# A hybrid decoder block on one core: pieces of work moved, another end, and two K steps of the second MLP product split earlier into general-pool tiles

## The chip, the core and the metric

The kernel runs on one core of one Trainium2 chip. The metric is the device time of one execution in microseconds, smaller is better. The engines of the core are named as in the profile: PE (TensorE, the matmuls), DVE (VectorE), ACT (ScalarE), POOL (GpSimd) and SP (SyncE, which here only issues DMAs). Operands that PE and the other engines work on lie in on-chip memory (SBUF), sums of products in PSUM; the rest moves by DMA.

## The reference

One layer of a pre-norm decoder block, on x of 1 x 2048 x 1024 in float32:

```python
h = rmsnorm(x, norm_mix_g)
u = h @ w_in                                   # 1024 -> 3*512 + 2*1024 columns
gate_b, gate_c, v, x_r, g = split(u)
y_conv = gate_b * causal_dwconv(gate_c * v, conv_w)            # width 512, 3 taps
xr = causal_dwconv(x_r, rnn_conv_w) + rnn_conv_b               # width 1024, 4 taps
y_rnn = rg_lru(xr, w_a, b_a, w_x, b_x, lru_lambda) * gelu(g)   # a scan over the sequence
y = concat(rmsnorm(y_conv, g_norm_conv), rmsnorm(y_rnn, g_norm_rnn))
x = x + y @ w_out                                              # 1536 -> 1024
h = rmsnorm(x, norm_mlp_g)
z = square(relu(h @ w_mlp_in))                                 # 1024 -> 4096
x = x + z @ w_mlp_out                                          # 4096 -> 1024
out = rmsnorm(x, final_norm_g)
```

## The kernel before

**Precision.** Every float32 operand of a large product is split into a high part (rounded to a shorter format, a cast on ACT, L172) and a low part (what is left, a subtraction on DVE, L173). A product is three matmuls: high by high, high by low, low by high. So each weight or operand tile of 128 x 1024 costs one cast of ACT and one subtraction of DVE before PE can use it. `round_off` and `split_new` do this.

**Blocks.** The sequence is four blocks of 512 rows, taken two at a time: `b` is 0 and then 2. Each pass has the stages mixers, `w_out` product, first MLP product ("up"), second MLP product ("down"). The pass with `b` = 0 computes the mixers with plain products (`mixers_plain`), the pass with `b` = 2 with block products (`mixers_blocks`). From the second pass on, and in both MLP products, the two blocks and two halves of the other sides are multiplied by a scheme of seven block products in place of eight: the products are numbered 1 to 7 and run in the order `ORDER = (1, 2, 6, 5, 7, 3, 4)`, with sums and differences of operands made on DVE. H1 to H7 are the operands of the first MLP product, made once per pass; `ops.put` makes H7, H3 and H4.

**Who sets the order.** The kernel is written for a framework that lays out each engine's instructions at build time: a planner takes them in the order of the program text as priority, as far as its own model finds them ready, and each engine then runs its list strictly in that order. Inside `tc.manual_schedule(engines=...)` the named engines keep the order of the text itself. PE is listed there from the `w_out` products on; in the mixers of the first pass it is not. `tc.issue_after(ins)` puts the instructions of its body behind `ins` on the same engine.

**Memory.** SBUF tiles come from pools with a fixed number of slots: the general pool (`temp`, 23 slots), the weight pool (`wtile`, 15 slots) and a pool of four wide tiles (`wide` and `duo`). A tile that finds no free slot waits for the last reader of an older one. PSUM has four tiles of 128 x 2 x 512.

**The places that the change touches, in order of time.**

- The start (`mixers_plain`, n = 0): row factors of the first norm are not applied to x before the product but to the product's result. `firsts[k].factors()` makes them for block k, `spread` turns them into a 128 x 512 tile with a diagonal (L362), a matmul with ones (L370) and a copy by ACT (L405); then `drain_x` and `drain_g` multiply the PSUM tiles by it (L720, L723).
- The end of the first mixers: `w_out_conv` multiplies the conv half of y, 4 row tiles per block. Between its tiles `during(t)` runs other work: for t = 0 it fetches the y of the second block (`fetch_y`), runs `between(0)`, which is the gate (sigmoids on ACT) and the scan of the last unit, and splits the fetched y (`conv_operands`, L652 and L653).
- The gate group of the second mixers (`InGate`): `refill_u` loads the tile `u1` from DRAM into a wide slot.
- The first MLP product: step n multiplies pair (s, i) of `seq`, `drain` takes it out of PSUM (L1065 to L1106) and spills z to DRAM; weights are prepared two steps ahead. The first six steps are i = 1 and 2 for s = 0, 1, 2; steps 6 to 10 are 6, 5, 7, 3, 4 of s = 0. In steps 2, 3 and 4 H7, H3 and H4 are made.
- The second MLP product: `Down.fetch` loads z and the weights of one of the 56 K steps, `prepare` splits them, `multiply` runs 24 matmuls. The first two are prepared in the last two steps of the first product, behind their drains, into weight-pool tiles.
- The end (`b` = 2): the last two K steps are multiplied row tile by row tile; each tile is added to x (L1549), squared and summed by ACT (L1206), its factor is made by `rstd_of` and both halves are scaled by DVE (L1220) and written out.

Of the kernel before, what the change touches and what calls it, by code (L numbers as in the profile page):

```python
# [10 lines left out]
AF = mybir.ActivationFunctionType  # L11
# [3 lines left out]
P = 128  # L15
# [46 lines left out]
def block_kernel(  # L62
# [257 lines left out]
    def rstd_of(dst, v, n):  # L320
        a = small("rs_a")[:, :n]
        s = small("rs_s")[:, :n]
        q = small("rs_q")[:, :n]
        V.tensor_scalar(a, v, 1.0 / D, EPS, MUL, ADD)
        root = nc.scalar.activation(s, a, AF.Sqrt)
        V.reciprocal(s, s)
        if n == 1:
            V.scalar_tensor_tensor(q, s, a, s, MUL, MUL)
        else:
            V.tensor_mul(q, s, s)  # L330
            V.tensor_mul(q, q, a)
        V.tensor_scalar(q, q, -0.5, 1.5, MUL, ADD)
        V.tensor_mul(dst, s, q)
        return root.ins

    HALF = [slice(0, 512), slice(512, D)]

# [343 lines left out]
    def mixers_plain(h):  # L681
# [30 lines left out]
        for n in SEQUENCE:  # L712
            if n < 4:
                pr = n
                u0, u1 = Lru(2 * pr), Lru(2 * pr + 1)
                xin = new_xin(pr)
                g = wide("g")

                def drain_x(blk, ps):
                    V.tensor_mul(block(xin, blk, 3), ps, over(R, blk))  # L720

                def drain_g(blk, ps):
                    V.tensor_mul(block(g, blk), ps, over(R, blk))  # L723
                    nc.scalar.activation(block(g, blk), block(g, blk), AF.Gelu_apprx_tanh)

                if pr == 0:
                    pss = []
                    wg = both("g0", lambda blk, ps: pss.append(ps), (0,))
                    with tc.issue_after(prepare_second()):
                        for k in range(4):  # L730
                            firsts[0].part(k)
                    firsts[0].factors()
                    both("x0", lambda blk, ps: pss.append(ps), (1,), w_first)
                    psR = psum("bc")
                    firsts[0].spread(R[:, 0, :], psR[:, 0, :])
                    seen = nc.gpsimd.tensor_copy(warm, R[:, 0, 0:1]).ins
                    with tc.issue_after(seen):
                        for m, i, pair in held:
                            kept[m, i] = [spill_r("ws", t, nc.gpsimd) for t in pair]
                    split_kept = spilled[0]  # L740
                    drain_x(0, start_x)
                    for k in range(4):
                        firsts[1].part(k)
                    firsts[1].factors()
                    pss.append(
                        col_products(
                            "g0", wg, h[1], lambda: firsts[1].spread(R[:, 1, :], psR[:, 1, :])
                        )
                    )
                    drain_x(1, pss[1])  # L750
                    drain_g(0, pss[0])
                else:
                    around("x%d" % pr, drain_x, late)
                    wg = None
                gw = load_gate(pr)
                keep_halo(pr, xin)
                u0.conv(xin)
                if late:
                    late.out()
                if pr == 3:  # L760
                    fetched = [fetch_y(mix.ys["A"], q, 0) for q in range(2)]
                if pr:
                    wg = both("g%d" % pr, drain_g, (0,), take("g%d" % pr, 1 + pr // 3))
                u1.conv(xin)
                last = latest[0]
                if pr == 3:
                    keep_sums(n)
                    rA = stats(mix.acc["A"], 512, "A")
                if pr:
                    both("g%d" % pr, drain_g, (1,), wg)  # L770
                else:
                    drain_g(1, pss[2])
                if pr == 3:
                    ysA = conv_operands(fetched)
                if pr:
                    u0.gate(gw)
                    u0.scan()
                late = Late(mix, u0, u1, g, gw)
                if pr < 3:
                    with tc.issue_after(last), tc.issue_after(split_kept):  # L780
                        keep_sums(n)
                continue
            if n < 6:
                pr = n - 4
                if R2 is None:
                    R2 = temp("R2")
                    nc.scalar.activation(R2, R, AF.Square)
                gc = wide("gc")
                around(
                    "c%d" % pr,  # L790
                    lambda blk, ps: V.tensor_mul(block(gc, blk), ps, over(R2, blk)),
                    late,
                )
                if late:
                    late.out()
                    late = None
                cv = new_cv(pr)
                both(
                    "v%d" % pr,
                    lambda blk, ps: V.tensor_mul(block(cv, blk, 2), ps, block(gc, blk)),  # L800
                )
                u = conv_short(pr, cv)
                for blk in range(2):
                    V.tensor_mul(block(u, blk), block(u, blk), over(R, blk))
                us[pr] = spill("u", u, nc.gpsimd)
                for k in range(4):
                    nxt[pr].part(k)
                nxt[pr].factors()
            else:
                for pr in range(2):  # L810
                    u = refill_u(us[pr])
                    around(
                        "b%d" % pr, lambda blk, ps: V.tensor_mul(block(u, blk), ps, block(u, blk)), late
                    )
                    if late:
                        late.out()
                        late = None
                    mix.conv(u)
            keep_sums(n)
# [109 lines left out]
    class InGate(In):  # L929

        def drain(self, i):
# [15 lines left out]
            elif i == 2:  # L947
                gated(self.u0, 0, plus(block(self.t, 0), self.y))
            elif i == 6:
                self.u1 = refill_u(self.us[1])  # L950
                snap(block(self.t, 1), self.x)
            elif i == 5:
                snap(block(self.t, 0), self.w)
            elif i == 7:
                gated(self.u1, 1, plus(block(self.t, 0), self.x))
# [176 lines left out]
    class Down:  # L1132
# [14 lines left out]
            else:  # L1147
                load(t, W2[a, i])

        def prepare(self, i, a):  # L1150
            self.ready[i, a] = (
                split_new(self.z.pop((i, a)), wtile, "z"),
                split_new(self.w.pop((i, a)), wtile, "w"),
            )

        def multiply(self, i, a, ts=range(NT)):
# [48 lines left out]
            sq = temp("sq", (P, TB))  # L1205
            nc.scalar.activation(sq, x_half(b, t, i), AF.Square, accum_out=ss[:, i : i + 1])  # L1206

    def finish_tile(b, t, gfin, ss=None, queues=None):
        rs = small("rs")[:, 0:1]
        if ss is None:  # L1210
            ss = small("ss")
            finish_squares(b, t, ss, range(2))
        else:
            finish_squares(b, t, ss, (0,))
        V.tensor_add(ss[:, 0:1], ss[:, 0:1], ss[:, 1:2])
        rstd_of(rs, ss[:, 0:1], 1)
        r0 = b * TB + t * P
        for i, sl in enumerate(HALF):
            xv = x_half(b, t, i)
            V.scalar_tensor_tensor(xv, xv, rs, gfin[:, sl], MUL, MUL)  # L1220
            (queues or (nc.gpsimd, nc.gpsimd))[i].dma_start(outf[r0 : r0 + P, sl], xv)

    def finish(b):
        gfin = gain(final_norm_g)
# [112 lines left out]
    for b in range(0, NB, 2):  # L1337
# [8 lines left out]
        with tc.manual_schedule(engines={nc.tensor.engine}):  # L1346
# [1 line left out]
            ahead = 0 if b else 1  # L1348
            ws = [take("oA0", ahead), take("oA1", ahead)]

            nextA = []

            def during(t):
                if t == 0:
                    nextA.extend(fetch_y(mix.ys["A"], q, 1) for q in range(2))
                between(t)
                if t == 0:
                    ysA.extend(conv_operands(nextA))
                if t == 2:
                    load_unit(cursor[0])  # L1360
# [75 lines left out]
        with tc.manual_schedule(engines={nc.tensor.engine}):  # L1436
# [6 lines left out]
            for n in range(-LEAD1, len(seq)):  # L1443
# [19 lines left out]
                    continue  # L1463
                s, i = seq[n]
                ups[s].multiply(i, ops.H)
                ups[s].drain(i, Z)
                if more and n > 7 and n % 3 == 2:
                    w2_sums(n // 3 - 2)
# [1 line left out]
                    rest(2, xs[0])  # L1470
                if n == 1:
                    rest(3, xs[1])
                if n == 2:
                    for q in range(2):
                        V.tensor_tensor(raw1[q], raw1[2 + q], raw1[q], SUB)
                    ops.put(ops.begin(7), raw1[:2])
                if n == 3:
                    ops.put(ops.begin(3), raw1[2:])
                if n == 4:
                    ops.put(ops.begin(4), raw0[2:])  # L1480
                if s == NS - 1 and i in (5, 7, 3, 4):
                    m = (5, 7, 3, 4).index(i)
                    if m < FETCH2:
                        down.fetch(*dseq[m], Z)
                    if i in (3, 4):
                        down.prepare(*dseq[i - 3])

            R = None
            for n in range(len(dseq) - (0 if more else 2)):
# [50 lines left out]
            if not more:  # L1540
                gfin = gain(final_norm_g)
                ends = [small("ss") for _ in range(NT)]
                for t in range(NT):
                    finish_squares(b + 1, t, ends[t], (1,))
                for t in range(NT):
                    for i, a in dseq[-2:]:
                        down.multiply(i, a, (t,))
                    xv = x_half(b + 1, t, 0)
                    V.tensor_add(xv, down.x[t // 2][:, t % 2], xv)  # L1549
                    finish_tile(b + 1, t, gfin, ends[t], (nc.sync, nc.scalar))  # L1550
        if more:
            finish(b + 1)
            ops = ops2
# [57 lines left out]
```

## Time and profile before

| | us |
|---|---|
| median of 3 runs | 2160.62 (2160.02 to 2161.12) |
| profiled execution | 2160.86 |
| its span, first to last instruction | 2159.1 |
| granted clock of PE, mean | 0.996 of full speed |

A line of the timeline gives start and duration in microseconds, engine (a q behind it means its sequencer), source line, operation, what is written from what, shape and count, and in brackets the idle time of the engine before it and what ended that. A line of the waits gives who waited for whom, the total in microseconds, how often, and the longest. A line of the stretches gives start and end, length, busy time and instructions of PE, PE's weight loads, DVE, ACT and POOL, the granted clock of PE, the DMA share and GB/s. A line of the DMA issues ends with the size of one and the median time from issue to landing.

### The profile page before, as it was taken

To read this page: it belongs to the slowest core of one execution; us is meant where nothing else is said; L and a number is where in the kernel's file an instruction comes from. 1 tells how busy PE (TensorE), PEld (TensorE's weight loads), DVE (VectorE), ACT (ScalarE), POOL (GpSimd) and SP (SyncE) were. 2 spreads that over 40 slices of the span, in tenths; PEclk is the share of its full clock that TensorE was granted. 3 is DMA by queue.
4 is the path that set the end of the run, shared out by engine and by line. 5 is a ranking of instruction groups with operands and counts; after the bars stand their busy time and mean duration, and the time that the engine had idled before them with its cause. 6 is when DMAs were issued, how large, how long until landed. Compare 5 with 4: busy or idle time off the path is not lost. (4 is left out here: it accounts for less than half of the span.)

```text
span 2159.1 us, 25110 instructions
## 1 busy us (share of the span) xinstructions
PE 2125.7 (98%) x9488; PEld 1745.3 (81%) x9488; DVE 1481.7 (69%) x1726; ACT 966.7 (45%) x1218; POOL 184.8 (9%) x335
## 2 busy tenths in 40 slices
PE   9999999999999999999999999999999999999998
PEld 7888887887888878888887887778888888888886
DVE  5887877569787876577746567595886665644456
ACT  6745537354333234453536447474533233433333
POOL 1121210000111100000121121000000000000000
PEclk9999999999999999999999999999999999999999
DMA  8755755342887789699573574654144444876431
GB/s 294 292 201 211 279 188 176 128 156 95 298 307 257 285 335 409 260 401 336 191 256 107 189 265 159 241 185 166 49 161 161 156 156 176 338 290 228 157 137 78
DMA packets 180904, 472.51 MB, mean 219 GB/s; under 512 B 15664, under 2 KB 62768, under 8 KB 179760
## 3 DMA queue, kind: packets, MB, share of 16 engines
q1 hardware_dynamic: 141104, 328.30, 42.0%
q0 software_dynamic: 36800, 133.19, 16.5%
q10 hardware_dynamic: 2880, 9.44, 1.2%
q8 instruction: 74, 1.21, 0.2%
q14 instruction: 46, 0.38, 0.0%
HBM read 308.33 MB, written 162.53 MB: 218 GB/s over the span
## 5 line engine op out<-in xcount | busy, mean ns | idle before, releaser
L870 PE MATMUL up<-H,w_hi 128*128 128x512 f32 x1792 | 552.5, 390 | 4.2 <-DVE snap L1078 3.4
L173 DVE TENSOR_TENSOR w_lo<-w,w_hi 128x1024 fp32r<-128x1024 f32 x208 | 253.2, 1222 | 273.8 <-issue 170.9
L870 PEld LDWEIGHTS up<-H,w_hi 128*128 128x128 f32 x1792 | 335.6, 188 | 74.8 <-ACT H L172 4.2
L1172 PE MATMUL dn<-w_lo,z_hi 128*128 128x512 f32 x896 | 348.8, 389 | 2.0 <-DVE w_lo L173 2.0
L1172 PE MATMUL dn<-w_hi,z_hi 128*128 128x512 f32 x896 | 349.2, 390 | 1.6 <-DVE x L1549 1.6
L870 PE MATMUL up<-H,w_lo 128*128 128x512 f32 x896 | 348.6, 389 | 0.0
L1172 PE MATMUL dn<-w_hi,z_lo 128*128 128x512 f32 x896 | 348.6, 389 | 0.0
L172 ACT CAST z_hi<-z 128x1024 fp32r<-128x1024 f32 x112 | 117.9, 1053 | 260.9 <-PE dn L1172 244.7
L172 ACT CAST w_hi<-w 128x1024 fp32r<-128x1024 f32 x208 | 216.0, 1049 | 30.2 <-DVE w L1051 14.6
L870 PE MATMUL in<-H,wr 128*128 128x512 f32 x888 | 203.2, 390 | 0.4 <-ACT g L892 0.4
L1172 PEld LDWEIGHTS dn<-w_lo,z_hi 128*128 128x128 f32 x896 | 168.2, 188 | 38.0 <-DVE w_lo L173 2.8
L1172 PEld LDWEIGHTS dn<-w_hi,z_hi 128*128 128x128 f32 x896 | 168.2, 188 | 37.8 <-DVE x L1549 2.4
L870 PEld LDWEIGHTS up<-H,w_lo 128*128 128x128 f32 x896 | 168.2, 188 | 35.2
L1172 PEld LDWEIGHTS dn<-w_hi,z_lo 128*128 128x128 f32 x896 | 168.2, 188 | 34.6
L870 PEld LDWEIGHTS in<-H,wr 128*128 128x128 f32 x888 | 166.4, 188 | 36.0 <-ACT g L892 0.8
L173 DVE TENSOR_TENSOR z_lo<-z,z_hi 128x1024 fp32r<-128x1024 f32 x112 | 136.6, 1219 | 19.9 <-ACT z_hi L172 18.6
L1065 ACT COPY snap<-up 128x1024 f32<-128x1024 f32 x48 | 48.8, 1016 | 184.6 <-PE up L870 184.6
L258 PE MATMUL po<-w_hi,y_hi 128*128 128x512 f32 x384 | 122.1, 400 | 4.0 <-ACT w_hi L172 3.0
L258 PE MATMUL po<-w_hi,y_lo 128*128 128x512 f32 x384 | 120.0, 394 | 3.3 <-DVE y_lo L653 3.3
L258 PE MATMUL po<-w_lo,y_hi 128*128 128x512 f32 x384 | 119.9, 394 | 0.2 <-DVE w_lo L173 0.2
L173 DVE TENSOR_TENSOR w_lo<-raw,w_hi 128x1024 fp32r<-128x1024 f32 (+1 forms) x62 | 73.1, 1186 | 47.9 <-issue 25.3
L172 ACT CAST w_hi<-raw 128x1024 fp32r<-128x1024 f32 (+1 forms) x62 | 62.7, 1019 | 88.4 <-PE ps_x L235 23.8
(265 smaller groups left out, 3088.7 us busy)
## 6 DMA issues: line engine op xcount, KB each, us to landing
z<-d_z SPq DMA_DIRECT2D x112, 512.0 KB, 7.4
w<-in_w_mlp_out_dram SPq DMA_DIRECT2D x80, 512.0 KB, 6.1
wr<-d_ws POOLq DMA_DIRECT2D x74, 512.0 KB, 6.4
w<-in_w_mlp_in_dram SPq DMA_DIRECT2D x64, 512.0 KB, 4.9
d_z<-snap SPq DMA_DIRECT2D x64, 512.0 KB, 3.0
w<-d_w SPq DMA_DIRECT2D x64, 512.0 KB, 4.7
d_z<-z SPq DMA_DIRECT2D x48, 512.0 KB, 2.9
d_ws<-w_hi POOLq DMA_DIRECT2D x37, 512.0 KB, 6.8
```

The source lines that it names most:

```text
L172: nc.scalar.copy(hi, src)
L173: latest[0] = V.tensor_tensor(lo, src, hi.bitcast(F32), SUB).ins
L258: nc.tensor.matmul(ps[:, half, :], ys[:, j, t * P : (t + 1) * P], ws[j][:, 0, half * 512 : (half + 1) * 512], start=first and i == 0, stop ...
L870: nc.tensor.matmul(ps[:, j, :], ws[:, k, j * P : (j + 1) * P], hs(k), start=i in (1, 2, 5) and k == 0 and n == 0, stop=k == 3 and n == len ...
L1065: nc.scalar.copy(t, ps)
L1172: nc.tensor.matmul(ps[t // 2][:, t % 2, :], zs[:, p, t * P : (t + 1) * P], ws[:, p, :], start=i in (1, 2, 5) and a == 0 and p == 0 and n == 0,
```

## The change

Six edits.

1. In the start, the spread of block 0's factors is issued in the middle of block 1's x0 product instead of behind it.
2. In the first pass, the conv operands of the second block are split ahead of `between(0)` instead of behind it; in the second pass the order stays.
3. In `InGate`, `u1` is refilled at product 5 instead of product 6.
4. H7, H3 and H4 are made in steps 3, 5 and 6 instead of 2, 3 and 4.
5. The first two K steps of the second MLP product are both prepared behind the last multiply of i = 3 and ahead of its drain, in tiles of the general pool.
6. The end: the second halves of x are multiplied by the gain, and their sums of squares divided by D, ahead of the last products. The row tiles go in the order 0, 2, 1, 3, with ACT, DVE and PE in the order of the text. The scaling of a tile stands behind the square of the next one: the second half by ACT, the first by DVE, both written from SP's queue, the last tile's second half from ACT's.

```diff
+    def root_of(dst, a):
+        s = small("rs_s")[:, 0:1]
+        q = small("rs_q")[:, 0:1]
+        nc.scalar.activation(s, a, AF.Sqrt)
+        V.reciprocal(s, s)
+        V.scalar_tensor_tensor(q, s, a, s, MUL, MUL)
+        V.tensor_scalar(q, q, -0.5, 1.5, MUL, ADD)
+        V.tensor_mul(dst, s, q)
...
-                    both("x0", lambda blk, ps: pss.append(ps), (1,), w_first)
                     psR = psum("bc")
-                    firsts[0].spread(R[:, 0, :], psR[:, 0, :])
+                    pss.append(
+                        col_products(
+                            "x0",
+                            w_first,
+                            h[1],
+                            lambda: firsts[0].spread(R[:, 0, :], psR[:, 0, :]),
+                        )
+                    )
...
             elif i == 6:
-                self.u1 = refill_u(self.us[1])
                 snap(block(self.t, 1), self.x)
             elif i == 5:
+                self.u1 = refill_u(self.us[1])
                 snap(block(self.t, 0), self.w)
...
-        def prepare(self, i, a):
+        def prepare(self, i, a, new=wtile):
             self.ready[i, a] = (
-                split_new(self.z.pop((i, a)), wtile, "z"),
-                split_new(self.w.pop((i, a)), wtile, "w"),
+                split_new(self.z.pop((i, a)), new, "z"),
+                split_new(self.w.pop((i, a)), new, "w"),
             )
...
+    def end_tile(b, t, gfin, ss, final):
+        rs = small("rs")[:, 0:1]
+        a = small("rs_a")[:, 0:1]
+        V.scalar_tensor_tensor(a, ss[:, 0:1], 1.0 / D, ss[:, 1:2], MUL, ADD)
+        root_of(rs, a)
+        r0 = b * TB + t * P
+        x0, x1 = (x_half(b, t, i) for i in range(2))
+
+        def scale():
+            nc.scalar.activation(x1, x1, AF.Copy, scale=rs)
+            (nc.scalar if final else nc.sync).dma_start(outf[r0 : r0 + P, HALF[1]], x1)
+            V.scalar_tensor_tensor(x0, x0, rs, gfin[:, HALF[0]], MUL, MUL)
+            nc.sync.dma_start(outf[r0 : r0 + P, HALF[0]], x0)
+
+        return scale
...
                 if t == 0:
-                    nextA.extend(fetch_y(mix.ys["A"], q, 1) for q in range(2))
+                    nextA = [fetch_y(mix.ys["A"], q, 1) for q in range(2)]
+                    if not b:
+                        ysA.extend(conv_operands(nextA))
                 between(t)
-                if t == 0:
+                if t == 0 and b:
                     ysA.extend(conv_operands(nextA))
...
                 ups[s].multiply(i, ops.H)
+                if s == NS - 1 and i == 3:
+                    for m in range(2):
+                        down.prepare(*dseq[m], temp)
                 ups[s].drain(i, Z)
...
-                if n == 2:
+                if n == 3:
                     for q in range(2):
                         V.tensor_tensor(raw1[q], raw1[2 + q], raw1[q], SUB)
                     ops.put(ops.begin(7), raw1[:2])
-                if n == 3:
+                if n == 5:
                     ops.put(ops.begin(3), raw1[2:])
-                if n == 4:
+                if n == 6:
                     ops.put(ops.begin(4), raw0[2:])
...
-                    if i in (3, 4):
-                        down.prepare(*dseq[i - 3])
...
                     finish_squares(b + 1, t, ends[t], (1,))
-                for t in range(NT):
+                    x1 = x_half(b + 1, t, 1)
+                    V.tensor_mul(x1, x1, gfin[:, HALF[1]])
+                    V.tensor_scalar(ends[t][:, 1:2], ends[t][:, 1:2], 1.0 / D, EPS, MUL, ADD)
+        if not more:
+            order = (0, 2, 1, 3)
+            with tc.manual_schedule(
+                engines={nc.scalar.engine, nc.vector.engine, nc.tensor.engine}
+            ):
+                done = None
+                for t in order:
                     for i, a in dseq[-2:]:
                         down.multiply(i, a, (t,))
                     xv = x_half(b + 1, t, 0)
                     V.tensor_add(xv, down.x[t // 2][:, t % 2], xv)
-                    finish_tile(b + 1, t, gfin, ends[t], (nc.sync, nc.scalar))
+                    finish_squares(b + 1, t, ends[t], (0,))
+                    if done:
+                        done()
+                    done = end_tile(b + 1, t, gfin, ends[t], t == order[-1])
+                done()
```

More of the change, by code (lines that the diff above doesn't have):

```diff
@@ L1206, in finish_squares, with finish_tile @@
             nc.scalar.activation(sq, x_half(b, t, i), AF.Square, accum_out=ss[:, i : i + 1])
-    def finish_tile(b, t, gfin, ss=None, queues=None):
+    def finish_tile(b, t, gfin):
         rs = small("rs")[:, 0:1]
[L1210 to L1214, printed above, removed]
+        ss = small("ss")
+        finish_squares(b, t, ss, range(2))
         V.tensor_add(ss[:, 0:1], ss[:, 0:1], ss[:, 1:2])
@@ L1220, in finish_tile @@
             V.scalar_tensor_tensor(xv, xv, rs, gfin[:, sl], MUL, MUL)
-            (queues or (nc.gpsimd, nc.gpsimd))[i].dma_start(outf[r0 : r0 + P, sl], xv)
+            nc.gpsimd.dma_start(outf[r0 : r0 + P, sl], xv)
+    def end_tile(b, t, gfin, ss, final):
[11 more added lines that the diff above has]
+        return scale
     def finish(b):
@@ L1349, in block_kernel @@
             ws = [take("oA0", ahead), take("oA1", ahead)]
-            nextA = []
             def during(t):
                 if t == 0:
-                    nextA.extend(fetch_y(mix.ys["A"], q, 1) for q in range(2))
+                    nextA = [fetch_y(mix.ys["A"], q, 1) for q in range(2)]
+                    if not b:
+                        ysA.extend(conv_operands(nextA))
                 between(t)
-                if t == 0:
+                if t == 0 and b:
                     ysA.extend(conv_operands(nextA))
```

## The prediction

> **What bounds the kernel now.** I read the page first, then the waits of TensorE (PE) over the whole span, then the timeline around each of them.
>
> ```profile
> span 2159.1 us, 25110 instructions
> PE 2125.7 (98%) x9488; PEld 1745.3 (81%) x9488; DVE 1481.7 (69%) x1726; ACT 966.7 (45%) x1218; POOL 184.8 (9%) x335
> ```
>
> PE is busy for all but 33 us. No product is removed by the diff, so whatever it brings must come out of those 33 us, out of stretches in which PE runs at a lower clock, or out of the tail behind the last matmul. The waits of PE (waiting line, releaser: us in total, times, longest) say where the 33 us lie:
>
> ```profile
> PE up L870 <- DVE snap L1078: 3.4, 2, 1.7
> PE po L258 <- DVE y_lo L653: 3.3, 3, 1.9
> PE po L258 <- ACT w_hi L172: 3.0, 1, 3.0
> PE dn L1172 <- DVE w_lo L173: 2.0, 1, 2.0
> PE ps_g L235 <- DVE xr_in L720: 2.0, 1, 2.0
> ...
> PE dn L1172 <- DVE x L1549: 1.6, 2, 0.8
> PE in L870 <- ACT w_hi L172: 1.5, 1, 1.5
> ```
>
> Five of these rows are touched by the diff. The kernel is bound by PE everywhere else, so a microsecond taken out of a wait is a microsecond of the whole, unless the next tile is late too. That question is asked of each edit below.
>
> **The start: the spread ahead of the second half.** Before, the matmul that spreads the row factors (L370) stands behind the whole x0 product of block 1; the diff puts it at that product's middle.
>
> ```profile
> 31.89 0.88 DVE L362 TENSOR_SCALAR diag<-ident,rs_x 128x128 f32<-128x128 f32 x4
> ...
> 41.02 1.02 PE L370 MATMUL bc<-diag,ones 128*128 128x512 f32 x2
> 44.03 0.72 PE L235 MATMUL ps_g<-h,w_hi 128*128 128x512 f32 x2 [1.99 <-DVE xr_in L720]
> ...
> 45.30:48.70 3.40, 3.40 (x10) 2.66 (x9) 0.99 (x5) 2.01 (x2) 0.91 (x3) 0.51 0.99 384
> ```
>
> The diagonal is ready at 32.8 us, but the spread runs at 41.0. PE then waits 1.99 us for ScalarE's copy of it and for VectorE's x drain (L720), which gives back a PSUM tile. Half a product is 24 matmuls at 0.23 us from start to start (two such rows stand at the end below), some 5.4 us, so the moved spread runs near 35.6, after the diagonal, and copy and drain lie beside the second half. The wait goes: 1.99 us. The last row, one stretch with the granted clock third from the end, shows more: right behind the wait PE had 0.51 of its clock for 3.4 us. That is 3.4 x 0.49 = 1.67 us lost, and I count it with the wait: **3.7 us**. What the edit issues besides (one matmul pair, one copy, and behind the copy six spills on POOL's queue) is as before, only 5 us earlier. If the cover were gone, that is, if the diagonal came after 35.6, PE would stall in mid-product for what is missing; the margin is 2.8 us.
>
> [...] The trace has the half clock directly behind a gap of 1.99 us; the case in which it comes from something else is a rival below.
>
> **Conv operands before the gates (block 0 only).** The y of the second block are split after the last Lru's gate and scan.
>
> ```profile
> 356.29 0.71 ACT L652 ACTIVATE y_hi<-y,prm 128x512 fp32r<-128x512 f32 x1
> ...
> 363.15 0.73 PE L258 MATMUL po<-w_hi,y_lo 128*128 128x512 f32 x2 [1.88 <-DVE y_lo L653]
> ...
> y<-d_yA SPq DMA_DIRECT2D x4, 256.0 KB, 7.7
> ```
>
> ScalarE makes the first y_hi at 356, and PE waits three times for y_lo, 3.3 us in all. The same four y_hi (4 x 0.71) and four y_lo are made in both versions, so nothing is added; put ahead of the gate, they are done before PE wants them. What waits behind them is the gate's sigmoids on ScalarE, later by 4 x 0.71 = 2.8 us, and VectorE's scan behind these. The last y are loaded behind that scan, but the four y_hi no longer stand in its second half, so I take it as no later. The loads take 7.7 us to land; if ScalarE's queue has y_hi in front before the landing, the sigmoids stand behind it for as long. Bounds: 3.3 gained, or nothing. I take **3.3 us**, nearer to the row of the wait.
>
> **H7, H3, H4 later in the first MLP product.** One stretch, twice (at 510 and at 1565):
>
> ```profile
> 505.94 2.35 DVE L173 TENSOR_TENSOR H<-raw,H 128x1024 fp32r<-128x1024 f32 x2
> ...
> 509.35 1.22 DVE L1078 TENSOR_TENSOR snap<-up,snap 128x1024 f32<-128x1024 f32 x1
> ...
> 510.71 0.47 PE L870 MATMUL up<-H,w_hi 128*128 128x512 f32 x1 [1.70 <-DVE snap L1078]
> ```
>
> The drain L1078 frees the PSUM tile that PE wants at 509.0. Ahead of it in VectorE's queue stands the H7 split, 2.35 us that PE needs only at step 8. With H7 one step later the drain ends 2.35 us earlier, near 508.2, and the wait goes. H7 is then due at step 8 and made at step 3, H3 at 9 and 5, H4 at 10 and 6: three to five steps of 24 x 0.23 = 5.4 us in hand. **3.4 us** for both; the bound below is one of the two, 1.7.
>
> **Two K steps prepared ahead of the last drains.** VectorE, around the start of the second product:
>
> ```profile
> 783.16 0.69 DVE L1123 TENSOR_TENSOR w<-w,w 128x512 f32<-128x512 f32 x1 [3.04 <-DMA w<-in_w_mlp_out_dram]
> ...
> 785.51 1.22 DVE L173 TENSOR_TENSOR w_lo<-w,w_hi 128x1024 fp32r<-128x1024 f32 x1
> ...
> 796.16 1.22 DVE L173 TENSOR_TENSOR w_lo<-w,w_hi 128x1024 fp32r<-128x1024 f32 x1
> ...
> 801.32 1.22 DVE L173 TENSOR_TENSOR w_lo<-w,w_hi 128x1024 fp32r<-128x1024 f32 x1
> ...
> 799.09 1.05 ACT L172 CAST z_hi<-z 128x1024 fp32r<-128x1024 f32 x1 [5.41 <-DMA z<-d_z]
> ...
> 797.44 0.50 PE L1172 MATMUL dn<-w_lo,z_hi 128*128 128x512 f32 x1 [2.03 <-DVE w_lo L173]
> ```
>
> The second step's w_lo (796.16) comes behind the drains, and PE waits 2.03 us for it at 797.44, in the second matmul of the step. In tiles of the general pool (23 slots) instead of the weight pool (15) it need not wait for weight slots, and VectorE has 3.04 us idle just before. But the third step is next: its w_lo ends at 802.54, and PE wants it 24 matmuls after 797.44, at 802.9, or 800.9 without the wait. Its z is loaded by SP behind the spills of the drain, hence the 5.41 us that z_hi waits. With one split (1.22, the 785.51 row) moved from ahead of the drain into that idle time, that load is 1.2 us earlier and a wait of about 0.4 stays: **1.6 us**. Bounds: 2.0 above; below, if VectorE makes both splits of the second step (2.45) in front of the drain without using its idle time, the third step is ready at 805.0, a wait of 4.1, and the edit costs 2.1. In the second pass (1843) there is no wait to remove, and I take nothing.
>
> **The later refill of u1** frees SP's queue for what stands behind it. PE waits 1.5 us near there for a w_hi (the last of the waits above). The wait is for ScalarE's cast, and nothing I read puts it down to the load; I take 0, with 0 and 1.5 as bounds. Loaded later, u1 has two products, 48 matmuls, until it is used.
>
> **The new end.** The chain of work that ended last:
>
> ```profile
> 2140.68 5.79 PE dn L1172 x24
> ...
> 2147.24 3.05 PE dn L1172 x12
> ...
> 2150.31 0.69 DVE x L1549
> ...
> 2153.58 0.21 ACT rs_s L325
> ...
> 2154.65 0.75 DVE x L1220
> 2155.40 0.66 DVEq L1607
> ```
>
> ```profile
> 2139.28 0.39 PE L1172 MATMUL dn<-w_lo,z_hi 128*128 128x512 f32 x1
> 2139.51 0.39 PE L1172 MATMUL dn<-w_hi,z_lo 128*128 128x512 f32 x1
> 2139.93 0.69 DVE L1549 TENSOR_TENSOR x<-dn,x 128x512 f32<-128x512 f32 x1 [7.10 <-PE dn L1172]
> 2140.66 0.63 ACT L1206 ACTIVATE sq<-x 128x512 f32<-128x512 f32 x1 [12.55 <-DVE x L1549]
> 2141.20 0.19 ACT L1206 ACTIVATION_READ_ACCUMULATOR sq<-x 128x1 f32 x1
> ```
>
> Tiles 0 and 1 share a PSUM tile, as do 2 and 3, so PE waits twice for the add (the 1.6 row). In the order 0, 2, 1, 3 the add lies beside another tile's 12 matmuls (2.76 us), and PE ends at 2139.9 + 3 x 2.76 = 2148.2 and not 2150.3. Now VectorE and ScalarE set the end. A tile takes 0.70 for the add, 0.73 for the square with its read-out, 0.70 for ScalarE's scaling of the tile before (the y_hi row, same shape and function) and 1.07 from square root to factor (2153.58 to 2154.65), with hand-overs 3.27; the first has no scaling but a visible small operation, 2.79. So the factors are ready at 2142.7, 2146.0, 2149.3, 2152.5, and the two last halves, now side by side, end 0.75 later at 2153.3, against 2156.06: **2.8 us**. The added four multiplies by the gain (0.69 each, as L1549) lie in idle VectorE time before 2139.93 (the 7.10 of that row); uncovered they would cost 2.8. The two last writes start together; I leave the 3 us behind them. Bounds: 2.0, if the writes get in each other's way, and 3.7.
>
> **Sum.** 3.7 + 3.3 + 3.4 + 1.6 + 2.8 = 14.8 us. The profiled execution took 2160.86, its span 2159.1; the median of the runs is 2160.62, the same within 0.02%. 2160.9 - 14.8 = **2146.1**.
>
> **Rivals.**
>
> 1. The half clock is not the gap's doing.
> ```profile
> 393.50:396.50 3.00, 2.75 (x8) 2.20 (x8) 1.51 (x12) 0.21 (x1) 0.00 (x0) 0.50 0.10 40
> ```
> Here the clock is 0.50 though none of the waits listed above lies there. For it speaks this row; against it that at 45.3 the loss comes straight behind the wait. Then the start gives 2.0: 2147.8. [...]
>
> 2. The next tile is late. ScalarE stands in front of the y loads and the second product's third step takes the wait: no 3.3, and -2.1 in place of 1.6. For it: the 7.7 us and 5.41 us rows. 14.8 - 3.3 - 3.7 = 7.8: 2153.1.
>
> 3. The moves don't do what they say. The order on VectorE, ScalarE and SP is made by a planner, which may put each moved piece back where it was, or lose elsewhere what it wins. Only the end, whose order is written out, is left: 2158.1.
>
> 4. Slower. The planner's new order puts a weight cast behind another engine's wait in ScalarE's queue, as already happens before the conv output product:
> ```profile
> 1384.03 1.02 ACT L903 ACTIVATE g<-in 128x1024 f32<-128x1024 f32 x1 [8.94 <-PE in L870]
> ...
> 1386.90:1393.70 6.80, 6.49 (x15) 4.71 (x16) 4.88 (x5) 4.15 (x5) 0.00 (x0) 0.51 0.26 87
> ...
> 50.00:340.00 290.00, 290.00 (x1321) 236.02 (x1319) 230.65 (x225) 153.96 (x175) 49.80 (x85) 1.00 0.63 228
> ```
> The casts stood behind this; PE lost 3.0 us and then 6.8 x 0.49 = 3.3 of clock, 6.3 together. Three more such places eat 19 us: 2165.1. From the third it decides. Against it the last row: from 50 to 340 us, with many such casts, PE is never idle.
>
> **Chances.** Forecast 0.50, the rivals in order 0.12, 0.22, 0.09, 0.07. A measurement of this kernel can tell about 0.2%, 4.3 us. Faster by more: 0.50 + 0.12 + 0.22 = 0.84; within: 0.09; slower: 0.07. The range goes from 2142 (third step in time 0.4, the refill's 1.5, the end's 0.9, and the 393.5 stretch at full clock 1.5 on top) to 2154, past rival 2.
>
> **What would show it.** Right: no wait of ps_g on L720 and full clock at 45; none of po on y_lo near 360; none of up on L1078; dn's wait on w_lo at most 0.5; PE's last matmul about 2.2 us nearer to the tail's start and no wait on the add. Wrong: new rows of PE on ACT or DVE of over 1 us, above all dn on the third step's w_lo, po on gi L523, or a tail longer than 3 us after the last scaling.

## The result and the profile after

| | before | after |
|---|---|---|
| median, same chip | 2161.12 us (5 runs) | 2148.59 us (5 runs, 2144.50 to 2153.26) |
| profiled execution | 2160.86 us | 2148.59 us |
| its span | 2159.1 us | 2146.8 us |

The changed kernel is faster by 0.6%: ratio 0.994, 95% interval 0.9921 to 0.9958. A second set of five runs gave 2149.54 us against 2160.44, ratio 0.9955 (0.9941 to 0.9969). Two slow runs of that second set, one of before (3062.18 us) and one of the last version below (10861.57 us), are left out of the ratios. The forecast was 2146.1, the range 2142 to 2154. The page of after, its first lines, and the waits of PE (waiting line, releaser: us in total, times, longest); its lines are numbered anew, L870 is L885, L1078 is L1093, L1172 is L1187 and L1549 is L1588 now:

```profile
span 2146.8 us, 25095 instructions
...
PE 2125.4 (99%) x9488; PEld 1748.2 (81%) x9488; DVE 1481.0 (69%) x1726; ACT 971.7 (45%) x1224; POOL 184.3 (9%) x335
```

```profile
PE po L258 <- ACT w_hi L172: 3.0, 1, 3.0
...
PE in L885 <- ACT w_hi L172: 1.5, 1, 1.5
...
PE dn L1187 <- DVE w_lo L173: 0.9, 1, 0.9
...
PE po L258 <- DVE x L1259: 0.7, 1, 0.7
```

The same 9488 matmuls, and PE is as busy (2125.4 against 2125.7 us): the time came out of waits and the tail. Gone are up on the drain, po on y_lo, ps_g on xr_in and dn on the add; dn on w_lo is 0.9 and not 2.0. New is the last row.

PE runs the same number of matmuls in both kernels, so the n-th of before can be laid beside the n-th of after, and the difference of their starts says where the time went. I read it off the records at the edges of these stretches (clock of before):

| stretch of before, us | forecast | after | what it holds |
|---|---|---|---|
| 0 to 25 | 0 | +0.6 | first matmuls: 17 from 3 to 6 us, before 23 |
| 25 to 60 | -3.7 | -3.6 | spread |
| 342 to 384 | -3.3 | -3.1 | conv operands |
| 384 to 420 | 0 | +0.2 | |
| 420 to 520 | -1.7 | -2.0 | H7, first pass |
| 520 to 720 | 0 | -1.3 | one wait of 0.7 on a drain and one of 0.1, not there after |
| 720 to 812 | -1.6 | -1.0 | two K steps |
| 812 to 1420 | 0 | +1.8 | half clock near 1310 |
| 1420 to 1470 | 0 | +1.6 | half clock near 1443 |
| 1470 to 1580 | -1.7 | -2.0 | H7, second pass |
| 1580 to 2100 | 0 | -0.3 | |
| 2100 to the end | -2.8 | -3.1 | end: PE -2.2, tail -0.9 |

The terms of the forecast add up to -14.8, and the same stretches of after to 3.6 + 3.1 + 2.0 + 1.0 + 2.0 + 3.1 = 14.8. The other stretches give back 2.6, mostly by half clock at two places that no edit touches. Stretches of before and of after (length, PE, PE's loads, DVE, ACT and POOL busy with counts, granted clock, DMA share, GB/s):

```profile
45.30:48.70 3.40, 3.40 (x10) 2.66 (x9) 0.99 (x5) 2.01 (x2) 0.91 (x3) 0.51 0.99 384
393.50:396.90 3.40, 3.15 (x9) 2.50 (x9) 1.51 (x12) 0.26 (x2) 0.00 (x0) 0.50 0.09 35
1386.90:1393.70 6.80, 6.49 (x15) 4.71 (x16) 4.88 (x5) 4.15 (x5) 0.00 (x0) 0.51 0.26 87
```

```profile
45.00:48.40 3.40, 3.40 (x17) 2.81 (x16) 1.34 (x7) 3.39 (x5) 0.53 (x1) 1.00 1.02 395
388.30:391.70 3.40, 3.40 (x10) 2.64 (x9) 1.30 (x12) 1.25 (x2) 0.00 (x0) 0.50 0.66 233
1309.90:1313.30 3.40, 3.23 (x8) 2.58 (x9) 1.53 (x3) 3.37 (x4) 0.00 (x0) 0.50 0.79 289
1378.20:1385.00 6.80, 6.12 (x14) 4.36 (x15) 5.25 (x5) 4.51 (x5) 0.00 (x0) 0.50 0.20 72
1443.00:1446.40 3.40, 3.40 (x10) 2.63 (x9) 3.40 (x12) 1.88 (x4) 0.00 (x0) 0.50 0.79 269
```

Before had 13.6 us at half clock, after 17.0; the 3.4 us at 45 us are gone, those at 1310 and 1443 have come. Each 3.4 us at 0.50 cost 1.7 us.

### The profile page after: what moved, and what is told of

Its sections match the earlier page's. It is cut to its first block, busy times and chain, and to the rows that moved or that the text cites. A ratio compares the mean times of both kernels' runs of the same rounds, so it can differ in the third digit from the quotient of the medians.

```text
span 2146.8 us, 25095 instructions
## 1 busy us (share of the span) xinstructions
PE 2125.4 (99%) x9488; PEld 1748.2 (81%) x9488; DVE 1481.0 (69%) x1726; ACT 971.7 (45%) x1224; POOL 184.3 (9%) x335
## 5 line engine op out<-in xcount | busy, mean ns | idle before, releaser
L885 PE MATMUL up<-H,w_hi 128*128 128x512 f32 x1792 | 552.2, 389 | 0.0
L885 PEld LDWEIGHTS up<-H,w_hi 128*128 128x128 f32 x1792 | 336.0, 188 | 69.2
L1187 PE MATMUL dn<-w_lo,z_hi 128*128 128x512 f32 x896 | 348.8, 389 | 0.9 <-DVE w_lo L173 0.9
L1187 PE MATMUL dn<-w_hi,z_hi 128*128 128x512 f32 x896 | 349.2, 390 | 0.0
L885 PE MATMUL up<-H,w_lo 128*128 128x512 f32 x896 | 348.7, 389 | 0.0
L1187 PE MATMUL dn<-w_hi,z_lo 128*128 128x512 f32 x896 | 348.7, 389 | 0.0
L885 PE MATMUL in<-H,wr 128*128 128x512 f32 x888 | 203.1, 390 | 0.4 <-ACT g L907 0.4
L1187 PEld LDWEIGHTS dn<-w_lo,z_hi 128*128 128x128 f32 x896 | 168.2, 188 | 36.5 <-DVE w_lo L173 1.3
L1187 PEld LDWEIGHTS dn<-w_hi,z_hi 128*128 128x128 f32 x896 | 168.2, 188 | 35.4 <-ACT w_hi L172 0.2
L885 PEld LDWEIGHTS up<-H,w_lo 128*128 128x128 f32 x896 | 168.2, 188 | 35.1
L1187 PEld LDWEIGHTS dn<-w_hi,z_lo 128*128 128x128 f32 x896 | 168.2, 188 | 34.6
L885 PEld LDWEIGHTS in<-H,wr 128*128 128x128 f32 x888 | 166.4, 188 | 36.0 <-ACT g L907 0.9
```

What stands on the lines that cost most here:

```text
L885: nc.tensor.matmul(ps[:, j, :], ws[:, k, j * P : (j + 1) * P], hs(k), start=i in (1, 2, 5) and k == 0 and n == 0, stop=k == 3 and n == len ...
L1187: nc.tensor.matmul(ps[t // 2][:, t % 2, :], zs[:, p, t * P : (t + 1) * P], ws[:, p, :], start=i in (1, 2, 5) and a == 0 and p == 0 and n == 0,
```

## The experiments

The theory was that of the forecast: each edit takes a wait of PE away, and half clock follows the wait. The rivals were that the edits don't act alone (pool against place), that a wait only moves, and that half clock belongs to the place and not to the wait. Each part but the refill was undone by itself, then two further edits were tried. In what follows "the stretch" is the difference against before in one stretch of the table.

**The spread, undone.**

```diff
-                    pss.append(col_products("x0", w_first, h[1], lambda: firsts[0].spread(...)))
+                    both("x0", lambda blk, ps: pss.append(ps), (1,), w_first)
+                    firsts[0].spread(R[:, 0, :], psR[:, 0, :])
```

> The changed kernel with the spread of the first row factors put back behind the whole x0 product. Theory (the wait and the clock behind it were both the spread's): PE waits about 2.0 us for the x drain at some 44 us again; every PE instruction from 60 us on is 2.0 us later than in the changed kernel if the clock stays full, 3.7 us if PE gets half of its clock for 3.4 us right behind the wait. Rival (the half clock at 45 us of the kernel before had nothing to do with the wait): the 2.0 us come back and the clock at 45 us is full. Rival (the change hides the wait only because of the new order elsewhere): no wait at 44 us.

2150.3 us, span 2148.5. PE's timeline:

```profile
44.84 0.73 PE L235 MATMUL ps_g<-h,w_hi 128*128 128x512 f32 x2 [1.99 <-DVE xr_in L729]
```

The wait is back to the hundredth, but the clock stayed full (1.00 from 44.00 to 48.40): the stretch 25 to 60 is -1.6 where after has -3.6. So the edit is worth 2.05 us of wait; the other 1.6 was before's half clock, which this execution didn't have with the same wait. The third K step waited longer too (1.9 on w_hi and 0.9 on w_lo); that is taken up with the K steps below.

**The conv operands, undone.**

```diff
-                    if not b:
-                        ysA.extend(conv_operands(nextA))
                 between(t)
-                if t == 0 and b:
+                if t == 0:
                     ysA.extend(conv_operands(nextA))
```

> The changed kernel with the conv operands of the second block split behind the gate and scan again, in both passes. Theory: three waits of PE on y_lo near 356 us come back, 3.3 us, and the new wait of 0.7 us on the adds (po on DVE x, at 349.7) goes, net 2.6 to 2.8 us later from 370 us on. Rival (the waits went because PE came 3.3 us earlier or the planner's order changed elsewhere): they stay away, under 1 us of difference.

2149.01 us, span 2147.2. The waits on y_lo are back, the new wait on x L1259 is gone, and half clock stands behind the wait of 1.9 (the row 359.91 below). The stretch 342 to 384 is +1.2 against -3.1 of after: 4.3 us, 1.7 of them half clock, so 2.6 of waits.

**H7, H3 and H4 one to two steps earlier.**

```diff
-                if n == 3:
+                if n == 2:
...
-                if n == 5:
+                if n == 3:
...
-                if n == 6:
+                if n == 4:
```

> The changed kernel with the H7, H3 and H4 operands put back one to two steps earlier (made at steps 2, 3 and 4 of the first MLP product instead of 3, 5 and 6). Theory (the wait of up on the drain came from the H7 split that stood ahead of that drain on VectorE): the two waits of up on the snap drain (1.7 us each, near 503 and 1557 us) come back, and the span is 3.4 us longer than the changed kernel's 2146.8, i.e. 2150.2. Rival (other moves of the change had already cleared VectorE there, or the wait only shifts slack that a later wait of the same pass gives back): no such wait, or a later wait of PE in the same pass is shorter by as much, span within 1 us of 2146.8.

2152.07 us, span 2150.3, as expected. VectorE's order, here and in after:

```profile
499.95 2.35 DVE L173 TENSOR_TENSOR H<-raw,H 128x1024 fp32r<-128x1024 f32 x2
502.22 1.21 DVE L173 TENSOR_TENSOR w_lo<-w,w_hi 128x1024 fp32r<-128x1024 f32 x1
503.36 1.21 DVE L1093 TENSOR_TENSOR snap<-up,snap 128x1024 f32<-128x1024 f32 x1
```

```profile
499.99 1.22 DVE L1093 TENSOR_TENSOR snap<-up,snap 128x1024 f32<-128x1024 f32 x1
...
503.39 2.35 DVE L173 TENSOR_TENSOR H<-raw,H 128x1024 fp32r<-128x1024 f32 x2
```

With H7 and one w_lo in front, the drain starts 3.4 us later. The row "PE up L885 <- DVE snap L1093: 3.4, 2, 1.7" is back, and the stretches 420 to 520 and 1470 to 1580 are both 0.0 where after has -2.0.

**The two K steps: pool, place, and both.** The general pool but the old place, the new place but the weight pool, and both undone:

```diff
-                if s == NS - 1 and i == 3:
-                    for m in range(2):
-                        down.prepare(*dseq[m], temp)
...
+                    if i in (3, 4):
+                        down.prepare(*dseq[i - 3], temp)
```

> The changed kernel with the two K steps prepared behind the drains again, as before, but in tiles of the general pool. Theory (the place): PE waits about 2.0 us on the second step's w_lo near 786 us, and not on the third's; net 1.1 us later than the changed kernel from 800 us on. Rival (the pool): 0.9 us on the third step as in the changed kernel, no difference.

```diff
-                        down.prepare(*dseq[m], temp)
+                        down.prepare(*dseq[m])
```

> The changed kernel with the two early K steps split into tiles of the weight pool, at the same place in the text. Theory (the place is what matters): both steps are still split before the last drains on DVE; PE waits at the start of the second product 0.5 to 1.5 us, as in the changed kernel with its 0.9. Rival (the pool is what matters): the wait of 2.0 us on the second step's w_lo is back, or a longer one, because the split waits for weight slots.

```diff
-                        down.prepare(*dseq[i - 3], temp)
+                        down.prepare(*dseq[i - 3])
```

> The changed kernel with the first two K steps of the second MLP product prepared as before: behind the last drains and in tiles of the weight pool (both halves of that part undone; the kernel that undid the place alone lost 11 us). Theory A (the part is worth about what the trace of before lost there): the 2.0 us wait of dn on the second step's w_lo near 790 us is back, the third step's 0.9 us wait goes, no wait in the second pass, span 2147.9 to 2149. Theory B (it is the place that counts, whatever the pool): the first step waits 4 us and more in both passes, with half clock behind it, and the span is 2155 or more.

The last diff stands against the first of the three, the others against the changed kernel. Their times are 2159.87, 2150.48 and 2148.30 us. PE's timeline at the second product, general pool in the old place:

```profile
782.77 0.65 PE L1187 MATMUL dn<-w_hi,z_hi 128*128 128x512 f32 x1 [4.08 <-ACT w_hi L172]
784.22 0.80 PE L1187 MATMUL dn<-w_lo,z_hi 128*128 128x512 f32 x1 [0.80 <-DVE w_lo L173]
```

Both undone, and after:

```profile
789.73 0.50 PE L1187 MATMUL dn<-w_lo,z_hi 128*128 128x512 f32 x1 [2.05 <-DVE w_lo L173]
```

```profile
792.65 0.50 PE L1187 MATMUL dn<-w_lo,z_hi 128*128 128x512 f32 x1 [0.95 <-DVE w_lo L173]
```

The pool is no gain by itself: in the old place it makes the first step wait, in both passes (8.2 us in two waits on w_hi), in the first with half clock behind it (the matmul at 782.77 took 0.65 us, where one of after took 0.39), and the stretches are +5.9 (720 to 812) and +7.5 (1580 to 1870). This is more than either expectation had; that the casts there wait for slots that the drains hold was not tried. The new place in the weight pool keeps the first two steps in time, but DVE makes the splits in between its drains, the last spill is 2 us later, and the third step waits 1.8 and 0.9 us, more than was expected. Both undone give the stretch 0.0 where after has -1.0, and -1.3 in its second profile.

What the third step waits for is read from after, by SP's queue and ACT:

```profile
782.73 0.32 SPq L131 DMA_DIRECT2D d_z<-z  x1
783.10 0.45 SPq L141 DMA_DIRECT2D z<-d_z  x1
```

```profile
789.15 1.05 ACT L172 CAST z_hi<-z 128x1024 fp32r<-128x1024 f32 x1 [6.48 <-DMA z<-d_z]
```

Its z is loaded behind the last drain's spill, and the drain's time hangs on a load in turn. DVE waits 1.5 us for it in front of the sums of the weights, which stand ahead of that drain:

```profile
773.66 0.69 DVE L1138 TENSOR_TENSOR w<-w,w 128x512 f32<-128x512 f32 x1 [1.50 <-DMA w<-in_w_mlp_out_dram]
```

How long DVE waits for this load differs from profile to profile, and the third step's wait mostly grows with it. Seven profiles have this part unchanged and z fetched as in after. In five of them the load wait was 0.70 to 2.11 us and the stretch -1.4 to -0.4. It was longest with the spread undone and in the version of the conv product's splits below: 2.85 and 2.91 us, after which the third step waited 1.9 and 0.9 us in the one, 1.8 and 0.9 in the other, and the stretches are +1.9 and +1.4. The first of the two:

```profile
777.75 0.69 DVE L1132 TENSOR_TENSOR w<-w,w 128x512 f32<-128x512 f32 x1 [2.85 <-DMA w<-in_w_mlp_out_dram]
```

Before and the kernel with both halves undone waited 3.04 and 3.06 us for their load, at a stretch of 0.0. So the part gained 1.0 to 1.3 us in the two profiles of after, and lost where the load came late; a gain on the average of executions is not shown. Nor is it shown that the weight pool by itself loses, since its waits of 1.8 and 0.9 us stand in two profiles with the general pool as well. This term is the least certain of all.

**The end, undone** (before's `finish_tile` with tiles 0, 1, 2, 3).

```diff
-            order = (0, 2, 1, 3)
...
-                    done = end_tile(b + 1, t, gfin, ends[t], t == order[-1])
+                    finish_tile(b + 1, t, gfin, ends[t], (nc.sync, nc.scalar))
```

> The changed kernel with the old end (tiles in order 0, 1, 2, 3, one factor at a time, both halves scaled on VectorE, writes on SP's and ScalarE's queues). Theory (the end is worth 2.8 to 3.1 us: PE no longer waits twice 0.8 us for the add, and the last tile's two halves are scaled side by side): two waits of dn on the x add of 0.8 us return, the last matmul is about 1 to 2 us later and the tail behind it 9.2 us instead of 8.3; the span is 2149.6 to 2149.9. Rival (the writes at the end set it, so that the order doesn't matter): span within 1 us of 2146.8.

2148.03 us, span 2146.3: no longer than after. But its waits have

```profile
PE dn L1187 <- DVE x L1566: 1.6, 2, 0.8
```

again, the stretch from 2100 to the last matmul is 0.0 where after has -2.2, and the tail behind that matmul is 8.80 us and not 7.86. The end is worth 3.1 us; the granted clock of this execution was 0.996 where after's was 0.995: less half clock elsewhere hides it, by estimate 2.1 us of it (0.001 of 2147). Of a single execution the stretch can be compared, the total can't.

**The changed kernel once more.** No diff.

> The changed kernel once more, not a line different. [...] Rival (the half clock belongs to the places): the same stretches again, span within 0.5 us of 2146.8.

2149.54 us (2147.19 to 2152.12), profiled span 2145.4. The waits agree within 0.3 us, and yet the 3.0 us wait near 1378 is followed by 3.4 us of half clock in place of 6.8:

```profile
1375.50:1378.90 3.40, 0.41 (x2) 0.20 (x2) 2.08 (x3) 3.15 (x4) 0.00 (x0) 1.00 0.00 0
1378.90:1382.30 3.40, 3.02 (x7) 1.90 (x7) 3.40 (x5) 3.38 (x4) 0.00 (x0) 0.50 0.00 0
1382.30:1385.70 3.40, 3.40 (x16) 2.77 (x16) 1.20 (x2) 0.49 (x1) 0.00 (x0) 1.00 0.63 181
```

The three other places kept theirs (0.51 at 389.0, 1310.6 and 1440.3), so 3.4 us of 17.0 went: what this wait cost in clock differed between two executions of one program.

**The third step's z loaded ahead of the last drain's spills.**

```diff
                 if s == NS - 1 and i == 3:
+                    down.fetch(*dseq[2], Z)
...
-                    if m < FETCH2:
+                    if m < FETCH2 and m != 2:
```

> The changed kernel with the load of the third K step's z issued ahead of the last drain's spills instead of behind them. Theory (the third step of the second product waits because its z is loaded by SP right behind the last spill, 783.10 to 789.05 us): the z arrives about 3 us earlier, the 0.9 us wait of dn on w_lo near 792 goes, 1.1 us less from there on; the span without half-clock stretches 1.1 us shorter, which the median of the times may not show. Rival (the third step is late by VectorE's queue): the wait stays or moves to w_hi.

> The kernel with the early load of the third step's z once more, not a line different, for a second profile. In its five timed runs it was 2142.14 to 2147.92, median 2144.64, but the one that was profiled was its second slowest (2147.79), and there the wait had only moved from the third step (gone) to the fourth (0.9 us, near 799). Theory (when the loads land differs from execution to execution, and with it whether the fourth step waits): the fourth step's wait is under 0.5 us or gone this time, the third step's still gone, span 2141 to 2145. Rival (the wait always moves to the fourth step, and the gain of the timed runs comes from elsewhere): 0.9 us again near 799.

Median 2144.64 us (2142.14 to 2147.92), ratio 0.9933 (0.9920 to 0.9946), beside 2149.54 of the changed kernel's second set. The profile says less: the third step's wait is gone, and the fourth waits 0.9 us near 799. In the second profile (2148.65 us) it waits 0.7 and 0.9 there. The rival holds: the wait moves one step on. Where the gain of the timed runs comes from stays open. DVE waited 4.29 and 4.20 us for the weight load in these two profiles, and yet the stretch 720 to 812 was -0.7 and +1.5 (the second with half clock: at 800.40 matmuls follow each other by 0.43 us, in the first profile by 0.23); without the edit it was +1.9 and +1.4 at load waits of 2.85 and 2.91. So the edit may pay where that load is late; two profiles suggest it and don't show it.

**The conv product's weight splits of the second pass in the general pool.**

```diff
+        nm = units[u][0]
+        new = temp if nm[:2] == "oA" and splits_in_temp[0] else wtile
-        note_split(u, rs, [split_new(r, wtile, "w") for r in rs])
+        note_split(u, rs, [split_new(r, new, "w") for r in rs])
```

> The changed kernel with the weight splits of the second pass's conv output product (units oA) put in tiles of the general pool instead of the weight pool. Theory (their casts stand on ScalarE behind the gelu, which waits 8.9 us for PE, because they wait for weight slots, and because the planner takes that for their place): the casts move ahead of the gelu, the 3.0 us wait of po on w_hi near 1378 and the 6.8 us of half clock behind it (3.3 us lost) go, and the span is 3 to 6.3 us shorter, 2140.5 to 2143.8. Rival (the casts are kept there by something else, or general-pool tiles taken there hold up other work): the wait stays or moves, span 2146 or more.

2144.75 us, span 2142.8. ScalarE's timeline:

```profile
1365.61 1.99 ACT L172 CAST w_hi<-raw 128x1024 fp32r<-128x1024 f32 x2
...
1376.97 1.02 ACT L921 ACTIVATE g<-in 128x1024 f32<-128x1024 f32 x1 [5.70 <-PE in L888]
```

Two of the four casts now stand ahead of the gelu that waits for PE. The 3.0 us wait is gone, and with it its half clock, going by the stretch 1376 to 1420, which is -5.1 where after has -0.1, and by the granted clock (0.998, after 0.995). New waits of 0.7 (w_lo) and 1.1 (y_lo) give part of it back. The third step waited 1.8 and 0.9 us, as with the spread undone, so that isn't put down to this edit.

**Both further edits** (the two diffs above).

> The two edits together: the early load of the third step's z and the weight splits of the second pass's conv output product in tiles of the general pool. Theory: neither the third step's wait (0.9 to 2.7 us in the runs so far) nor the 3.0 us wait near 1378 with its 6.8 us of half clock is there; median 2141 to 2144 against the changed kernel's 2148.6, a gain of 4 to 7 us. Rival (the gain of the one look at the second edit was luck with half-clock stretches): within 2 us of the changed kernel in the same call.

Median 2143.84 us, ratio 0.9923 (0.9909 to 0.9937). Beside the changed kernel's second set it is 5.7 us faster, and the two intervals don't meet. Its profiled span is 2140.0; the longest waits of PE:

```profile
PE psri L521 <- DVE xr_lo L173: 1.8, 2, 1.0
PE in L888 <- ACT w_hi L172: 1.5, 1, 1.5
PE in L888 <- DVE w_lo L173: 1.4, 3, 0.8
```

No wait of the second product is left, and none of 3.0. This is the lowest median of all; from the early load alone (2144.64) it can't be told apart, as their intervals overlap.

## Why the prediction was right, and where its steps were off

**The sum held, the total by a margin.** The five terms measure 14.8 us in the profiled pair, as forecast. That it agrees to a tenth is luck: +0.6 (H7, H3, H4) and +0.3 (the end) set off -0.6 (two K steps), -0.2 and -0.1. What the sum left out is mostly half clock elsewhere, so 2148.6 and not 2146.1; the ten runs of the changed kernel lie between 2144.5 and 2153.3.

**The start.** Forecast 3.7, measured 3.6, and split as the working has it: 2.05 for the wait, the rest for the clock. But the spread did not run near 35.6:

```profile
39.57 1.02 PE L379 MATMUL bc<-diag,ones 128*128 128x512 f32 x2
...
42.59 0.73 PE L235 MATMUL ps_g<-h,w_hi 128*128 128x512 f32 x2
```

```profile
41.30 1.23 DVE L729 TENSOR_TENSOR xr_in<-start_x,R 128x1024 f32<-128x1024 f32 x1 [8.85 <-ACT R L414]
```

PE's list there is the planner's, which placed it 2.6 us, some 11 matmuls, from the product's end. The forecast's margin of 2.8 us was that of the diagonal ahead of the spread, and it has grown (32.45 to 39.57). The one that counts turned out to be the drain's: it ends at 42.53 and PE wants its tile at 42.59, 0.1 us in hand. The step "half a product is 24 matmuls, so it runs near 35.6" failed; the result stood by luck.

**The conv operands.** Forecast 3.3, measured 3.1 in the stretch. The step "I take it as no later" failed in part: three y_lo now stand in front of the drain of x.

```profile
346.90 2.07 DVE L662 SCALAR_TENSOR_TENSOR y_lo<-y,prm,y_hi 128x512 fp32r<-128x512 f32 x3
...
348.89 0.74 DVE L1259 SCALAR_TENSOR_TENSOR x<-po,yr_A,x 128x512 f32<-128x512 f32 x1
```

PE waits 0.70 us for it. That is the next tile of the second rival, at a fifth of its price. By the n-th matmuls the three old waits were worth 4.1 us and this one gives back 1.0, so the 3.3 came out near as the balance of two misses.

**H7, H3, H4.** Forecast 1.7 each, measured 2.0 each. The trace counts a wait from the modelled end of the matmul ahead, 0.39 us behind its start; the next one would have started after 0.23, so each wait costs 0.16 us more than its row says. The matmul behind the wait, 0.31 us to the next in before, costs 0.08 more.

**Two K steps.** Forecast 1.6 with a third-step wait of 0.4; the wait was 0.95 and the term 1.0 (1.3 in the second profile). The mechanism was named, its size off: the reckoning moved one split out of the drain's way, but the last drain hangs on the weight load ahead of it. With that load late the term has the other sign (-1.9 and -1.4 where 1.6 was forecast), near its lower bound of -2.1, so 1.0 is also a matter of luck.

**The refill.** It was put at 0, and the wait of 1.5 us on w_hi is in after as in before. The edit moved nothing that the traces show: SP issues the load of u between the same neighbours in both, at 1314.28 us in before and at 1304.39 in after, 9.9 us earlier as PE is there. It was not run by itself.

**The end.** Forecast 2.8, measured 3.1. The factors come every 2.9 us, not every 3.27, as the chain of after shows (start, length, what):

```profile
2136.37 0.16 DVE rs L343
2136.53 0.61 DVE x L1588
2137.17 0.72 ACT sq L1221 x2
2137.89 0.61 ACT x L1244
2138.51 0.10 ACT rs_s L339
...
2139.27 0.16 DVE rs L343
...
2142.36 0.75 DVE x L1246
```

As forecast, DVE and ACT set the end, not PE.

**The rivals.** The first (the half clock at 45 is not the gap's doing) is not settled: half clock stood behind the gap of 1.99 us in before, none behind the same gap with the spread undone, and none in after, which has no gap there. The forecast's certainty that the gap costs the clock falls with that. The second holds for 0.7 us and, in two of the profiles above, for the third step (1.8 to 1.9 and 0.9 us). The third and the fourth fall: the pieces moved (the spread less far than written), and no cast came to stand behind another engine's wait.

## What to carry to other kernels

Where one engine is busy for 98% of the time, lay its n-th instruction of one kernel beside the n-th of the other: each edit then has its own stretch, and totals of single executions, which here differ by some 9 us for one program, aren't needed. A wait that was removed was worth its length here (2.05 us for the spread), and in some executions half clock as well (1.6 us there). When work is moved ahead of a drain, look at what the drain's spill releases, and at which load that drain itself waits. Give moved splits a pool and a place together: the new pool in the old place lost 11 us here.

## What the runs showed of the hardware

Up to the last matmul, the stretches of half clock in before and after were 3.4 or 6.8 us long (the rows above). In one of them two matmuls of 512 columns took 0.85 us from start to start (after, 389.07 to 389.92 us), at full clock 0.46 (394.44 to 394.90). The same wait had half clock behind it in one execution and not in another. Two neighbouring rows each, around a wait of PE on y_lo of 1.9 us, in before and with the conv part undone:

```profile
359.37:362.78 3.41, 1.66 (x6) 1.05 (x6) 3.41 (x5) 3.19 (x4) 0.00 (x0) 1.00 0.75 198
362.78:366.19 3.41, 2.88 (x11) 2.10 (x12) 3.41 (x6) 1.06 (x1) 0.00 (x0) 1.00 0.95 350
```

```profile
356.50:359.91 3.41, 1.53 (x8) 0.92 (x6) 3.41 (x5) 2.48 (x3) 0.00 (x0) 1.00 0.92 293
359.91:363.32 3.41, 3.41 (x10) 2.63 (x9) 3.41 (x6) 1.06 (x1) 0.00 (x0) 0.50 0.80 271
```

The granted clock behind it was 1.00 in the first and 0.50 in the second. So it is at the start: behind its wait of 1.99 us before had 0.51 (the row 45.30 above), and with the spread undone the clock was full:

```profile
40.67:44.08 3.41, 2.17 (x8) 1.13 (x6) 0.53 (x1) 1.12 (x3) 0.49 (x2) 1.00 0.00 0
44.08:47.49 3.41, 2.65 (x12) 2.19 (x13) 3.02 (x8) 2.11 (x2) 2.81 (x6) 1.00 0.77 311
```

The waits of 1.5 and 0.5 us near 1310 had 3.4 us of half clock behind them in both profiles of after (0.50 and 0.51), and none in before (1.00 from 1300 to 1340). Near 390, behind 16 matmuls of a single column in 2.25 us with waits of 0.26 us between and after them, it was 0.50 or 0.51 for 3.4 us in before and in both profiles of after. That is the row of the first rival. What decides whether a wait is followed by half clock is not shown.

The spans of the profiled pair differ by 12.3 us, and without half clock (13.6 us of it in before, 17.0 in after, at half their length) by 14.0. The medians differ by 10.9 and 12.5 us. Where the other 1.5 to 3.1 us go stays open; the granted clock, 0.994 to 0.996 in the five runs of after, and the third step's wait, which differs from execution to execution, are candidates.
